# Later bank sums and rests, residual rows over two passes, and a dt chain in steps, in a Trainium2 decoder layer

## The chip, the cores and the metric

The kernel runs on one core of one Trainium2 chip. The metric is the device time of one launch in microseconds, the median of the runs. Before the change it is 1476.61 us (three runs, 1475.93 to 1481.21).

## The reference, cut to what matters

One layer for 1024 tokens of width 1024, all in float32. `h = layer_norm(x)`; one wide projection `h @ w_in` gives the pieces that feed two mixers side by side:

```python
y_a = (silu(z_a) * b_gate * conv3(c_gate * u)) @ w_a_out
xbc = silu(conv4(xbc) + bias);  dt = softplus(dt_raw + dt_bias)
y_s = ssd_chunked(xs, dt, -exp(a_log), bs, cs) + d_skip * xs     # state-space scan, chunks of 128
y_s = gated_group_rmsnorm(y_s, z_s, norm_s_g) @ w_s_out          # four groups of channels
mixed = sigmoid(g_a) * y_a + sigmoid(g_s) * y_s
out = layer_norm(2**0.25 * h + mixed @ w_o) * ln_g + ln_b
```

## The kernel before, in words

Each float32 product is made of three matmuls: an operand is split into a rounded part ("hi") and a rest ("lo"), and hi*hi, hi*lo and lo*hi add up in a PSUM bank (L786 to L788, L922 to L924). ScalarE writes the hi part of a weight block (`prep_hi`, L276), VectorE its lo part by a subtraction (`prep_lo`, through the helper `sub_split`, L106).

The work is one hand-written list of **items**, each one block product on TensorE. Items "p" are the input projection: pairs of 128-column blocks, seven products to a pair. The first three pairs are interleaved and make up the early part; from item 21 (`START`) on, pairs follow one another, and the steps of the scan are placed between them. Items "a" (16) multiply by `w_a`. Items "s" multiply by `w_s`: four groups g of eight products j, written (g, j) below, 24 matmuls of 128x512 each. For every j the four groups add up in the SBUF tile `acc[j]`. After the list comes the output projection with `w_o` (`project`), whose left operands `M[j, half]` are made from `acc[j]` in group 3; what follows the list is not pinned, and the compiler's scheduler may place it among the last items.

For each item n the main loop issues, in this order: the load of the raw weights of item n+5 on SP's queue (`fetch`, L225); hi of item n+3 and lo of item n+2; the product; what stands in `sums[n]`; what stands in `later[n]`. From `START` on `pin` fixes each engine's order to this order of writing. So an instruction that waits holds back all that is written behind it on its engine, and a DMA that waits for its buffer holds back the rest of its queue. There are three lo buffers and eight raw buffers.

What the change touches:

- `item_s` (L850) makes the product (g, j) in two banks of a ring of eight and then empties them: in group 1 by an addition into `acc` (L874), in group 2 by that addition, a product with the tile `sg` (L876) and the addition of `yg` (L877), for each half; in group 3 by L880 and L881, after which ScalarE and VectorE write M (L883, L106). This emptying is called E(g, j) below.
- `load_gy` (L814) loads `sg` and `yg` of product j+1 in product j of group 2; `prep_y` (L770, L772) loads the tiles `rb` and `gt` of a later left operand. These are 512 KB each, and all take buffers of one pool, tag "O", which has four; a load waits on SP's queue until one comes free.
- `prep_y` puts its work two items later: VectorE scales `gt` (L775), ScalarE writes the two hi halves (L764), VectorE the two rests (L106, in `halves`).
- `residual(s)` makes one of eight row blocks of `2**0.25 * h` again: SP loads `x` (L838); one item later ScalarE normalises it (L844), GpSimd multiplies and adds (L845, L846) and stores the row to DRAM through its own queue (L847). Two buffers take turns. Row j is made in product (1, j).
- `item_a` multiplies its two banks with `sga` (L804) and stores the tile one item later.
- `dt_values` makes softplus, the sums over each chunk (L482 to L488 on TensorE) and their exponentials. It is issued whole at item 19, in the early part.

Of the kernel before, what the change touches and what calls it, by code (L numbers as in the profile page):

```python
# [21 lines left out]
AF = mybir.ActivationFunctionType  # L22
ALU = mybir.AluOpType
# [5 lines left out]
KT = D // P  # L29
HALF = 512  # L30
# [15 lines left out]
def trunk_kernel(ctx: ExitStack, tc: tile.TileContext, x, w_in, w_dt, w_a, w_s, w_o, par, con,  # L46
# [58 lines left out]
    def sub_split(lo, full, hi, eng):  # L105
        return eng.tensor_tensor(lo, full, hi.bitcast(F32), ALU.subtract)  # L106
# [46 lines left out]
    def bank(tag, name):  # L153
        return pa.tile([P, HALF], F32, tag=tag, name=name, bufs={"U": 2, "yy": 2}.get(tag, 1))
# [15 lines left out]
    def post_unit(name):  # L170
        n_post[0] += 1
        return unit(POST[(n_post[0] - 1) % 28], name)
# [5 lines left out]
    def xp(i):  # L178
        return ("cv", T_X + 2 * i, T_X + 2 * i + 1)

    def zp(i):
        return ("zs", T_ZS + 2 * i, T_ZS + 2 * i + 1)
# [2 lines left out]
    gates = [("ga", T_GA + 2 * i, T_GA + 2 * i + 1) for i in range(4)]  # L185
    gates += [("gs", T_GS + 2 * i, T_GS + 2 * i + 1) for i in range(4)]
    EARLY = 3
    pairs = [zp(0), zp(1), ("cv", T_BM, T_CM), xp(0), gates[0], xp(1)]
    group_at = {0: len(pairs) - 1}
    for g in range(1, G):  # L190
        pairs += [("cv", T_BM + g, T_CM + g), *conv_pairs[2 * g - 2], xp(2 * g), zp(2 * g), *conv_pairs[2 * g - 1],
# [265 lines left out]
        V.tensor_tensor(v, v, trd3[:, :, H:].rearrange("p c h -> p h c"), ALU.add)  # L457
        V.tensor_tensor(v, v, db_t.unsqueeze(2).to_broadcast([P, H, NCH]), ALU.add)

    def dt_values():  # L460
        v, e, s1, s2 = (w4[0][:, i] for i in range(4))

        S.activation(e, v, AF.Abs)
        ex = S.activation(e, e, AF.Exp, bias=0.0, scale=-1.0)
        V.tensor_scalar(s1, e, 2.0, None, ALU.add)
        V.reciprocal(s2, s1)
        V.tensor_tensor(s1, e, s2, ALU.mult)
        V.tensor_tensor(s2, s1, s1, ALU.mult)
        V.tensor_scalar(e, s2, 2.0 / 17.0, 2.0 / 15.0, ALU.mult, ALU.add)
        for d in (13, 11, 9, 7, 5, 3, 1):  # L470
            V.tensor_tensor(e, e, s2, ALU.mult)
            V.tensor_scalar(e, e, 2.0 / d, None, ALU.add)
        V.tensor_tensor(e, e, s1, ALU.mult)
        V.tensor_scalar(v, v, 0.0, None, ALU.max)
        V.tensor_tensor(dt_t, v, e, ALU.add)

        with tc.issue_after(ex.ins):
            S.activation(al_t, al_t, AF.Exp)
        V.scalar_tensor_tensor(s1, dt_t, -1.0, al_t.unsqueeze(2).to_broadcast([P, H, NCH]), ALU.mult, ALU.mult)
        s1f = s1.rearrange("p h c -> p (h c)")  # L480
        pc1 = bank("tr", "pc1")
        PE.matmul(pc1[:, 0:256], lhsT=upper, rhs=s1f, start=True, stop=True)  # L482
        PE.matmul(pc1[:, 256:512], lhsT=slow, rhs=s1f, start=True, stop=True)
        cumf = cum_t.rearrange("p h c -> p (h c)")
        V.tensor_copy(cumf, pc1[:, 0:256])
        S.activation(dte_t.rearrange("p h c -> p (h c)"), pc1[:, 256:512], AF.Exp)
        pc2 = bank("st", "pc2")
        PE.matmul(pc2[:, 0:256], lhsT=ones, rhs=s1f, start=True, stop=True)  # L488
        S.activation(cdec_t.rearrange("p h c -> p (h c)"), pc2[:, 0:256], AF.Exp)
        for i in range(2):  # L490
            PE.transpose(pc2[:, 256 + i * P:256 + (i + 1) * P], cumf[:, i * P:(i + 1) * P], ident)
        ce = cv("ceT")
        cT, eT = (ce[:, i * 256:(i + 1) * 256].rearrange("p (i l) -> p i l", i=2) for i in range(2))
        V.tensor_copy(cT.rearrange("p i l -> p (i l)"), pc2[:, 256:512])
        S.activation(eT.rearrange("p i l -> p (i l)"), pc2[:, 256:512], AF.Exp)
        for i in range(2):
            rows = slice(i * 16, (i + 1) * 16)
            SP.dma_start(cum_d[rows, :].rearrange("h (c l) -> (h c) l", c=NCH), cT[:, i, :])
            SP.dma_start(ecum_d[rows, :].rearrange("h (c l) -> (h c) l", c=NCH), eT[:, i, :])

    kept, taken = {}, set()
# [252 lines left out]

    ya_raw, Y, acc, sga, M, WO = {}, {}, {}, {}, {}, {}

    def halves(s, k, src):

        for hf_i in range(2):
            u = Y[s, k, hf_i] = post_unit(f"{s}_{k}{hf_i}")
            part = src[:, hf_i * HALF:(hf_i + 1) * HALF]
            S.activation(u[:, 0, :], part, AF.Copy)  # L764
            sub_split(u[:, 1, :], part, u[:, 0, :], V)

    def prep_y(g, k):

        rb = otile(f"rb{g}_{k}")
        SP.dma_start(rb, rst_d[g].squeeze(0).partition_broadcast(P))  # L770
        y = otile(f"gt{4 * g + k}")
        SP.dma_start(y, gat_d[g][:, k, :])  # L772

        def work():
            V.scalar_tensor_tensor(y, y, pc(C_NG + 4 * g + k), rb, ALU.mult, ALU.mult)  # L775
            halves(f"y{g}", k, y)
        later.setdefault(now[0] + (2 if items[now[0]][0] == "s" else 1), []).append(work)

    n_bank = [0]
# [11 lines left out]
    abank = {}  # L791

    def item_a(j, kh, hi, lo):
        if kh == 0:
            sga[j] = otile(f"sga{j}")
            SP.dma_start(sga[j], sga_d[j])
        for hf_i in range(2):
            if kh == 0:
                abank[hf_i] = pbank(f"p_wa{j}_{hf_i}")
            for k in range(4):  # L800
                mm3(abank[hf_i], hi, lo, k, Y["a", 4 * kh + k, hf_i], kh == 0 and k == 0, kh == 1 and k == 3)
        if kh == 1:
            for hf_i in range(2):
                V.tensor_tensor(sga[j][:, hcols[hf_i]], abank[hf_i], sga[j][:, hcols[hf_i]], ALU.mult)  # L804
            later.setdefault(now[0] + 1, []).append(lambda: SP.dma_start(yag_d[j], sga[j]))
        elif 1 <= j < 7:
            prep_y((j - 1) // 4, (j - 1) % 4)

# [41 lines left out]
    def item_s(g, j, hi, lo):  # L850
        if g == 0:
            acc[j] = xtile(j, f"acc{j}") if j < 7 else cv("acc7")
        ps = [pbank(f"p_ws{g}_{j}_{i}") for i in range(2)]
        for hf_i in range(2):
            for k in range(4):
                mm3(ps[hf_i], hi, lo, k, Y[f"y{g}", k, hf_i], k == 0, k == 3)
        if g < 3 and j in (1, 3, 5, 7)[:4 if g < 2 else 2]:
            y_next = 4 * g + 6 + j // 2
            prep_y(y_next // 4, y_next % 4)
        if g == 1:  # L860
            residual(j)
        if g == 1 and j == KT - 1:
            load_gy(0)
        if g == 2 and j < KT - 1:
            load_gy(j + 1)
        if g == 2 and j == KT - 1 or g == 3 and j < KT - 1:
            load_gy((j + 1) % KT, ("sg",))
        for hf_i in range(2):
            sl = hcols[hf_i]
            part = acc[j][:, sl]  # L870
            if g == 0:
                S.activation(part, ps[hf_i], AF.Copy)
            elif g < 3:
                V.tensor_tensor(part, ps[hf_i], part, ALU.add)  # L874
                if g == 2:
                    V.tensor_tensor(part, part, gy["sg", j][:, sl], ALU.mult)  # L876
                    V.tensor_tensor(part, part, gy["yg", j][:, sl], ALU.add)  # L877
            else:
                sg = gy["sg", j][:, sl]
                V.tensor_tensor(sg, ps[hf_i], sg, ALU.mult)  # L880
                V.tensor_tensor(part, part, sg, ALU.add)  # L881
                u = M[j, hf_i] = post_unit(f"m{j}_{hf_i}")
                S.activation(u[:, 0, :], part, AF.Copy)  # L883
                sub_split(u[:, 1, :], part, u[:, 0, :], V)
        if g == 3:
            if j < 4:
                split_wo(j, 0, unit(POST[8 + j], f"wo{j}_0"))
            if 1 <= j < 5:
                split_wo(3 + j, 0, xtile(j - 1, f"wo{3 + j}_0", F32R, (P, 2, HALF)))
            if j == 5:  # L890
                for n, i, src in (("lg", 4, ln_g), ("lb", 5, ln_b)):
                    norm_t[n] = xtile(i, n)
                    SP.dma_start(norm_t[n], src.partition_broadcast(P))
# [73 lines left out]
    for n, it in enumerate(items):  # L967
        if it[0] == "p" and it[2] == 1:
            first_of[n] = it[1]
    START = 7 * EARLY  # L970
    for n, (kind, i, j) in enumerate(items):
        now[0] = n
        for k in range(n, n + LF + 1):
# [15 lines left out]
        if kind == "p":  # L989
            item_p(i, j, hi, lo)  # L990
            if n == 2 * EARLY - 1:
                dt_project(0)
                second_half()
            if n == 3 * EARLY - 1:
                quarter_sums()
            if n == 4 * EARLY + 1:
                dt_project(1)
                dt_turn()
            if n == START - 2:
                dt_values()  # L1000
            if n == START - 1:
                est.release()
                sd["p"] = tc.alloc_tile_pool(name="S", bufs=1, reuse_waits="tile")
        elif kind == "a":
            item_a(i, j, hi, lo)
        else:
            item_s(i, j, hi, lo)
        for f in sums.pop(n, ()):
            f()
        for f in later.pop(n, ()):  # L1010
# [138 lines left out]
```

## Time and profile before

| | before |
|---|---|
| median of three runs | 1476.61 us |
| the profiled execution's own time | 1475.75 us |
| its span, first to last instruction | 1473.9 us |
| mean granted TensorE clock | 0.983 |
| busy TensorE / VectorE / ScalarE / GpSimd | 95 / 69 / 49 / 33 % |

The profiled execution is 0.86 us below the median, and 1.85 us of its time lie outside the span. Times inside it count from the first instruction. PE is TensorE, PEld its weight loads, DVE VectorE, ACT ScalarE, POOL GpSimd, SPq the DMA issues of SP's queue. A group of instructions is named by its line, engine and tiles (output, then inputs); "x2" is two instructions in one line of the view. A bracket in the timeline says how long the engine stood idle before, and what ended that.

### The profile page before, as it was taken

What the parts mean: (1) busy time and instruction counts of PE and PEld (TensorE: products, weight loads), DVE (VectorE), ACT (ScalarE), POOL (GpSimd) and SP (SyncE); (2) the same over time, 40 slices, a digit from 0 to 9 for tenths busy, and PEclk for the clock granted to TensorE, in tenths of its full rate; (3) what the DMA queues carried; (4) which work ended last, traced back from release to release, by engine and by line L of the source; (5) the groups of instructions that cost most, each with busy time, mean ns of one, the idle gap of its engine ahead of it and who ended that gap; (6) DMA issues with size and microseconds to landing.
All of it is one profiled execution on the core that took longest, in us unless ns stands there. A gap on an engine that the chain in (4) does not pass through costs nothing.

```text
span 1473.9 us, 18618 instructions
## 1 busy us (share of the span) xinstructions
PE 1399.5 (95%) x6522; PEld 1104.6 (75%) x6522; DVE 1017.1 (69%) x1495; ACT 717.2 (49%) x1244; POOL 481.9 (33%) x374
## 2 busy tenths in 40 slices
PE   6999999999999999999999999999799998679997
PEld 4677878787777877778787777877588886457886
DVE  7977578877788787697877586675534347668843
ACT  3665466555665645665555665555521332102411
POOL 4012334534334453244444254343000007400054
PEclk9999999999999999999999999999999999889999
DMA  6022255463444545454654535454557445557431
GB/s 228 16 93 100 105 143 134 135 167 112 146 122 141 167 121 133 137 147 122 176 126 143 150 106 166 132 144 146 204 186 242 166 164 198 209 186 243 164 114 57
DMA packets 171901, 217.02 MB, mean 147 GB/s; under 512 B 11520, under 2 KB 116896, under 8 KB 171808
## 3 DMA queue, kind: packets, MB, share of 16 engines
q1 hardware_dynamic: 162128, 181.80, 42.2%
q10 hardware_dynamic: 8272, 29.81, 5.2%
q0 software_dynamic: 1408, 4.23, 0.8%
q8 instruction: 51, 0.84, 0.2%
q14 instruction: 42, 0.34, 0.1%
HBM read 160.97 MB, written 54.82 MB: 146 GB/s over the span
## 4 chain that ended last, share of the span: by engine, by line
PE 79%; DVE 9%; DMA 5%; ACT 2%; POOL 2%; issue 2%; ACTq 0%; POOLq 0%; SPq 0%; DVEq 0%
PE p L922 10%; PE p L924 10%; PE p L923 10%; PE pU L924 8%; PE pU L922 8%; PE pU L923 8%; PE ya L653 2%; PE p_wa L788 2%; PE p_wa L787 2%; PE p_wa L786 2%; PE p_wo L1043 2%; PE p_wo L1045 2%; PE p_wo L1044 2%; PE st L658 2%; PE yb L648 2%
## 5 line engine op out<-in xcount | busy, mean ns | idle before, releaser
L106 DVE TENSOR_TENSOR wlop<-raw_a,whip 128x512 fp32r<-128x512 f32 x210 | 180.7, 861 | 181.2 <-ACT whip L276 67.5
L276 ACT ACTIVATE whip<-raw_a 128x512 fp32r<-128x512 f32 x210 | 127.8, 622 | 43.7 <-issue 10.7
L922 PE MATMUL p<-b,whip 128*128 128x512 f32 x352 | 143.7, 409 | 4.1 <-DVE ob L931 4.1
L922 PE MATMUL pU<-t,whip 128*128 128x512 f32 x352 | 144.5, 412 | 2.7 <-ACT oa L957 2.7
L922 PE MATMUL p<-t,whip 128*128 128x512 f32 x352 | 141.7, 403 | 1.5 <-DVE oa L931 1.5
L924 PE MATMUL p<-t,wlop 128*128 128x512 f32 x352 | 139.1, 395 | 1.5 <-DVE wlop L106 1.5
L923 PE MATMUL p<-b,whip 128*128 128x512 f32 x352 | 139.8, 397 | 0.1
L924 PE MATMUL pU<-t,wlop 128*128 128x512 f32 x352 | 138.9, 395 | 1.0 <-DVE wlop L106 1.0
L924 PE MATMUL p<-b,wlop 128*128 128x512 f32 x352 | 139.6, 397 | 0.0
L923 PE MATMUL pU<-t,whip 128*128 128x512 f32 x352 | 138.9, 395 | 0.0
L923 PE MATMUL p<-t,whip 128*128 128x512 f32 x352 | 138.9, 394 | 0.0
L788 PE MATMUL p_ws<-y,wlos 128*128 128x512 f32 x256 | 106.6, 417 | 32.6 <-DVE wlos L106 32.5
L638 POOL TENSOR_TENSOR xw<-xd,dte_t 128x256 f32<-128x256 f32 x56 | 46.5, 830 | 257.1 <-DVE xd L624 257.1
L786 PE MATMUL p_ws<-y,whis 128*128 128x512 f32 x256 | 105.0, 410 | 0.0
L787 PE MATMUL p_ws<-y,whis 128*128 128x512 f32 x256 | 104.4, 408 | 0.0
L236 POOL TENSOR_TENSOR s<-raw_a,raw_a 128x512 f32<-128x512 f32 x42 | 69.8, 1662 | 86.4 <-DVE wlop L106 73.7
L250 POOL TENSOR_TENSOR raw_a<-raw_a,s 128x512 f32<-128x512 f32 x42 | 65.9, 1570 | 97.9 <-issue 89.8
L106 DVE TENSOR_TENSOR wlop<-s,whip 128x512 fp32r<-128x512 f32 x84 | 80.2, 966 | 11.8 <-PE p L924 8.7
L922 PEld LDWEIGHTS p<-b,whip 128*128 128x128 f32 x352 | 66.7, 190 | 27.1 <-issue 8.6
L788 PEld LDWEIGHTS p_ws<-y,wlos 128*128 128x128 f32 x256 | 50.6, 198 | 48.6 <-DVE wlos L106 36.6
L604 ACT ACTIVATE em<-em,cum_t 128x128 f32<-128x128 f32 x256 | 81.3, 390 | 7.0 <-ACT ob L548 4.1
L922 PEld LDWEIGHTS pU<-t,whip 128*128 128x128 f32 x352 | 66.0, 187 | 19.9 <-ACT oa L957 4.0
(224 smaller groups left out, 3321.2 us busy)
## 6 DMA issues: line engine op xcount, KB each, us to landing
raw_a<-in_w_in_dram SPq DMA_DIRECT2D x168, 256.0 KB
em<-cum_d SPq DMA_DIRECT2D x64, 256.0 KB
xg_d<-cv ACTq DMA_DIRECT2D x16, 512.0 KB
xT<-xg_d SPq DMA_DIRECT2D x32, 256.0 KB
z<-zs_d SPq DMA_DIRECT2D x32, 256.0 KB
gat_d<-y SPq DMA_DIRECT2D x32, 256.0 KB
rb<-rst_d SPq DMA_DIRECT2D x16, 512.0 KB
gt<-gat_d SPq DMA_DIRECT2D x16, 512.0 KB
```

Source lines behind the costliest of these rows:

```text
L106: return eng.tensor_tensor(lo, full, hi.bitcast(F32), ALU.subtract)
L236: Gp.tensor_tensor(s1, r["a21"], r["a22"], ALU.add)
L250: Gp.tensor_tensor(a12, a12, s1s[p]["s2"], ALU.subtract)
L276: S.activation(flat(hi), src, AF.Copy)
L604: S.activation(em[:, h, :], em[:, h, :], AF.Relu, bias=cum_t[:, 8 * g + 4 * i + h, c:c + 1], scale=-1.0)
L638: Gp.tensor_tensor(xw, XD[n, i], dte_t[:, hs, c].unsqueeze(2).to_broadcast([P, HG, HD]), ALU.mult)
L786: PE.matmul(ps, lhsT=hi[:, k, :], rhs=u[:, 0, :], start=start, stop=False)
L787: PE.matmul(ps, lhsT=hi[:, k, :], rhs=u[:, 1, :], start=False, stop=False)
L788: PE.matmul(ps, lhsT=lo[:, k, :], rhs=u[:, 0, :], start=False, stop=stop)
L922: PE.matmul(ps, lhsT=hi[:, k, :], rhs=u[:, 0, :], start=first, stop=False, skip_group_check=True)
L923: PE.matmul(ps, lhsT=hi[:, k, :], rhs=u[:, 1, :], start=False, stop=False, skip_group_check=True)
L924: PE.matmul(ps, lhsT=lo[:, k, :], rhs=u[:, 0, :], start=False, stop=(k == 3), skip_group_check=True)
```

## The change

The third of the first six pairs becomes a pair of gates and the B/C pair takes the next place. `dt_values` becomes a generator with steps, one per item from item 21 on. `halves` can issue its two rests one item later, and `prep_y` asks for that. The product with `sga` in `item_a` and the emptying in `item_s` move into `sums` of the next item, except for the last product, (3, 7), which is still emptied in its own; the store of `sga` moves one item on as well. `residual` is called in every other product of groups 1 and 2 in place of every product of group 1.

```diff
@@ -185 +185 @@
-    pairs = [zp(0), zp(1), ("cv", T_BM, T_CM), xp(0), gates[0], xp(1)]
+    pairs = [zp(0), zp(1), gates[0], ("cv", T_BM, T_CM), xp(0), xp(1)]
@@ -460 +460 @@
-    def dt_values():
+    def dt_steps():
         v, e, s1, s2 = (w4[0][:, i] for i in range(4))
...
         S.activation(e, v, AF.Abs)
-        ex = S.activation(e, e, AF.Exp, bias=0.0, scale=-1.0)
+        S.activation(e, e, AF.Exp, bias=0.0, scale=-1.0)
+        S.activation(al_t, al_t, AF.Exp)
+        yield
...
+        yield
-        for d in (13, 11, 9, 7, 5, 3, 1):
+        for i, d in enumerate((13, 11, 9, 7, 5, 3, 1)):
             V.tensor_tensor(e, e, s2, ALU.mult)
             V.tensor_scalar(e, e, 2.0 / d, None, ALU.add)
+            if i % 2:
+                yield
...
+        yield
+        yield
-        pc1 = bank("tr", "pc1")
+        pc1, pc2 = bank("tr", "pc1"), bank("st", "pc2")
...
+        yield
...
@@ -759 +765 @@
-    def halves(s, k, src):
+    def halves(s, k, src, rest_later=False):
+        parts = [src[:, hf_i * HALF:(hf_i + 1) * HALF] for hf_i in range(2)]
+        us = [post_unit(f"{s}_{k}{hf_i}") for hf_i in range(2)]
         for hf_i in range(2):
...
+            Y[s, k, hf_i] = us[hf_i]
+            S.activation(us[hf_i][:, 0, :], parts[hf_i], AF.Copy)
+        def rests():
+            for u, part in zip(us, parts):
+                sub_split(u[:, 1, :], part, u[:, 0, :], V)
+        if rest_later:
+            later.setdefault(now[0] + 1, []).append(rests)
+        else:
+            rests()
...
-            halves(f"y{g}", k, y)
+            halves(f"y{g}", k, y, True)
@@ -800 +814 @@
         if kh == 1:
-            for hf_i in range(2):
-                V.tensor_tensor(sga[j][:, hcols[hf_i]], abank[hf_i], sga[j][:, hcols[hf_i]], ALU.mult)
-            later.setdefault(now[0] + 1, []).append(lambda: SP.dma_start(yag_d[j], sga[j]))
+            banks = dict(abank)
+            def gate():
+                for hf_i in range(2):
+                    V.tensor_tensor(sga[j][:, hcols[hf_i]], banks[hf_i], sga[j][:, hcols[hf_i]], ALU.mult)
+            sums.setdefault(now[0] + 1, []).append(gate)
+            later.setdefault(now[0] + 2, []).append(lambda: SP.dma_start(yag_d[j], sga[j]))
@@ -857 +875 @@
-        if g == 1:
-            residual(j)
+        if g in (1, 2) and j % 2 == 0:
+            residual(4 * (g - 1) + j // 2)
...
-        for hf_i in range(2):
-            sl = hcols[hf_i]
-            part = acc[j][:, sl]
+        def evac():
+            for hf_i in range(2):
+                sl = hcols[hf_i]
+                part = acc[j][:, sl]
...
+        if g == 3 and j == KT - 1:
+            evac()
+        else:
+            sums.setdefault(now[0] + 1, []).append(evac)
@@ -996 +1020 @@
-            if n == START - 2:
-                dt_values()
...
+        if n == START - 1:
+            dt_work = dt_steps()
+        if n >= START and dt_work is not None and n != first_cv:
+            if next(dt_work, "done") == "done":
+                dt_work = None
         for f in sums.pop(n, ()):
             f()
```

## Rows read from the trace of the kernel before

**Rows 1.** The page: busy time, share of the span and instructions of TensorE and VectorE.
```profile
PE 1399.5 (95%) x6522; PEld 1104.6 (75%) x6522; DVE 1017.1 (69%) x1495; ACT 717.2 (49%) x1244; POOL 481.9 (33%) x374
```

**Rows 2.** Whom TensorE waited for, whole run: total us, times, longest us.
```profile
PE p_ws L788 <- DVE wlos L106: 32.5, 8, 10.9
...
PE pc L482 <- DVE w L479: 2.8, 1, 2.8
```

**Rows 3.** Busy time by stretch, items "s" alone: us, busy by engine, clock, DMA.
```profile
1153.46:1243.06 89.60, 89.60 (x384) 72.19 (x384) 8.06 (x12) 9.57 (x16) 1.00 0.51 174
1243.06:1379.17 136.11, 101.81 (x385) 78.52 (x383) 21.69 (x32) 0.00 (x0) 0.87 0.61 210
```

**Rows 4.** Whom SP's queue waited for, 1190 to 1350 us.
```profile
SPq L838 <- DMA res_d<-rs: 56.4, 6, 21.9
```

**Rows 5.** Timeline of SP's queue: start, us, line, transfer.
```profile
1202.01 0.43 SPq L225 DMA_DIRECT2D raw_s<-in_w_s_dram  x1
1224.36 0.33 SPq L838 DMA_DIRECT2D rs<-in_x_dram  x1
...
1266.49 1.02 SPq L814 DMA_DIRECT2D sg<-sgs_d  x1
```

**Rows 6.** Timeline of VectorE in group 2.
```profile
1274.04 1.47 DVE L876 TENSOR_TENSOR acc<-acc,sg 128x512 f32<-128x512 f32 x1 [9.31 <-DMA sg<-sgs_d]
...
1280.23 0.68 DVE L106 TENSOR_TENSOR wlos<-raw_s,whis 128x512 fp32r<-128x512 f32 x1
...
1295.82 0.69 DVE L877 TENSOR_TENSOR acc<-acc,yg 128x512 f32<-128x512 f32 x1 [1.08 <-DMA yg<-yag_d]
...
1298.48 0.69 DVE L106 TENSOR_TENSOR wlos<-raw_s,whis 128x512 fp32r<-128x512 f32 x1
```

**Rows 7.** The chain that ended last: start, us waited for the landing, transfer.
```profile
1266.49 7.46 DMA sg<-sgs_d
...
1290.90 4.83 DMA yg<-yag_d
...
1298.59 5.51 DMA yg<-yag_d
```

**Rows 8.** Timeline of GpSimd and VectorE where residual rows are made.
```profile
1254.56 2.91 POOL L845 TENSOR_TENSOR rs<-rs,ag 128x1024 f32<-128x1024 f32 x1 [1.40 <-ACT rs L844]
1255.91 4.91 DVE L106 TENSOR_TENSOR y<-gt,y 128x512 fp32r<-128x512 f32 x2 [0.70 <-ACT y L764]
1257.55 2.73 POOL L846 TENSOR_TENSOR rs<-rs,ab 128x1024 f32<-128x1024 f32 x1
...
1263.65 2.74 POOL L846 TENSOR_TENSOR rs<-rs,ab 128x1024 f32<-128x1024 f32 x1
1264.06 0.68 DVE L874 TENSOR_TENSOR acc<-p_ws,acc 128x512 f32<-128x512 f32 x1
```

**Rows 9.** Groups of GpSimd, 1030 to 1380 us: count, busy us, mean ns, idle before.
```profile
L846 POOL TENSOR_TENSOR rs<-rs,ab 128x1024 f32<-128x1024 f32 x8 | 22.3, 2784 | 0.6
L845 POOL TENSOR_TENSOR rs<-rs,ag 128x1024 f32<-128x1024 f32 x8 | 19.6, 2450 | 185.1 <-ACT rs L844 185.1
```

**Rows 10.** Timeline: the steps between an emptied bank and a residual row.
```profile
1242.86 1.24 ACT L844 ACTIVATE rs<-rs,nb_t,rs_t 128x1024 f32<-128x1024 f32 x1 [0.32 <-DMA rs<-in_x_dram]
...
1287.60 1.28 DVE L775 SCALAR_TENSOR_TENSOR gt<-gt,par_t,rb 128x1024 f32<-128x1024 f32 x1
...
1288.91 1.15 ACT L764 ACTIVATE y<-gt 128x512 fp32r<-128x512 f32 x2 [15.85 <-DVE gt L775]
```

**Rows 11.** Timeline of VectorE: the lo parts of (3, 3) and (3, 7).
```profile
1344.64 0.68 DVE L106 TENSOR_TENSOR wlos<-raw_s,whis 128x512 fp32r<-128x512 f32 x1
...
1373.02 0.69 DVE L106 TENSOR_TENSOR wlos<-raw_s,whis 128x512 fp32r<-128x512 f32 x1
```

**Rows 12.** Busy time by stretch, VectorE alone, around the dt chain.
```profile
93.00:112.20 19.20, 17.35 (x33) 1.00 0.25 97
```

**Rows 13.** Busy time by stretch, all engines (TensorE, loads, VectorE, ScalarE, GpSimd), group 2.
```profile
1257.00:1304.00 47.00, 31.80 (x120) 24.22 (x120) 27.43 (x29) 5.71 (x8) 15.11 (x9) 0.85 0.61 216
```

More of the change, by code (lines that the diff above doesn't have):

```diff
@@ L458, in dt_turn @@
         V.tensor_tensor(v, v, db_t.unsqueeze(2).to_broadcast([P, H, NCH]), ALU.add)
-    def dt_values():
+    def dt_steps():
         v, e, s1, s2 = (w4[0][:, i] for i in range(4))
+        s1f = s1.rearrange("p h c -> p (h c)")
+        cumf = cum_t.rearrange("p h c -> p (h c)")
         S.activation(e, v, AF.Abs)
-        ex = S.activation(e, e, AF.Exp, bias=0.0, scale=-1.0)
+        S.activation(e, e, AF.Exp, bias=0.0, scale=-1.0)
+        S.activation(al_t, al_t, AF.Exp)
+        yield
         V.tensor_scalar(s1, e, 2.0, None, ALU.add)
@@ L475, in dt_values @@
         V.tensor_tensor(dt_t, v, e, ALU.add)
-        with tc.issue_after(ex.ins):
-            S.activation(al_t, al_t, AF.Exp)
         V.scalar_tensor_tensor(s1, dt_t, -1.0, al_t.unsqueeze(2).to_broadcast([P, H, NCH]), ALU.mult, ALU.mult)
-        s1f = s1.rearrange("p h c -> p (h c)")
-        pc1 = bank("tr", "pc1")
+        yield
+        yield
+        pc1, pc2 = bank("tr", "pc1"), bank("st", "pc2")
         PE.matmul(pc1[:, 0:256], lhsT=upper, rhs=s1f, start=True, stop=True)
         PE.matmul(pc1[:, 256:512], lhsT=slow, rhs=s1f, start=True, stop=True)
-        cumf = cum_t.rearrange("p h c -> p (h c)")
+        PE.matmul(pc2[:, 0:256], lhsT=ones, rhs=s1f, start=True, stop=True)
         V.tensor_copy(cumf, pc1[:, 0:256])
         S.activation(dte_t.rearrange("p h c -> p (h c)"), pc1[:, 256:512], AF.Exp)
-        pc2 = bank("st", "pc2")
-        PE.matmul(pc2[:, 0:256], lhsT=ones, rhs=s1f, start=True, stop=True)
         S.activation(cdec_t.rearrange("p h c -> p (h c)"), pc2[:, 0:256], AF.Exp)
+        yield
         for i in range(2):
@@ L495, in dt_values @@
         S.activation(eT.rearrange("p i l -> p (i l)"), pc2[:, 256:512], AF.Exp)
+        yield
         for i in range(2):
@@ L499, in dt_values @@
             SP.dma_start(ecum_d[rows, :].rearrange("h (c l) -> (h c) l", c=NCH), eT[:, i, :])
+        yield
     kept, taken = {}, set()
@@ L757, in trunk_kernel @@
     ya_raw, Y, acc, sga, M, WO = {}, {}, {}, {}, {}, {}
-    def halves(s, k, src):
+    def halves(s, k, src, rest_later=False):
+        parts = [src[:, hf_i * HALF:(hf_i + 1) * HALF] for hf_i in range(2)]
+        us = [post_unit(f"{s}_{k}{hf_i}") for hf_i in range(2)]
         for hf_i in range(2):
[L762 to L765, printed above, removed]
+            Y[s, k, hf_i] = us[hf_i]
[7 more added lines that the diff above has]
+            rests()
     def prep_y(g, k):
@@ L867, in item_s @@
             load_gy((j + 1) % KT, ("sg",))
-        for hf_i in range(2):
-            sl = hcols[hf_i]
-            part = acc[j][:, sl]
[L871 to L884, printed above, removed]
+        def evac():
+            for hf_i in range(2):
+                sl = hcols[hf_i]
+                part = acc[j][:, sl]
+                if g == 0:
+                    S.activation(part, ps[hf_i], AF.Copy)
+                elif g < 3:
+                    V.tensor_tensor(part, ps[hf_i], part, ALU.add)
+                    if g == 2:
+                        V.tensor_tensor(part, part, gy["sg", j][:, sl], ALU.mult)
+                        V.tensor_tensor(part, part, gy["yg", j][:, sl], ALU.add)
+                else:
+                    sg = gy["sg", j][:, sl]
+                    V.tensor_tensor(sg, ps[hf_i], sg, ALU.mult)
+                    V.tensor_tensor(part, part, sg, ALU.add)
+                    u = M[j, hf_i] = post_unit(f"m{j}_{hf_i}")
+                    S.activation(u[:, 0, :], part, AF.Copy)
+                    sub_split(u[:, 1, :], part, u[:, 0, :], V)
+        if g == 3 and j == KT - 1:
+            evac()
+        else:
+            sums.setdefault(now[0] + 1, []).append(evac)
         if g == 3:
@@ L970, in trunk_kernel @@
     START = 7 * EARLY
+    dt_work, first_cv = None, -1
     for n, (kind, i, j) in enumerate(items):
```

## The prediction

> **What bounds the kernel now.** I read the page first, then TensorE's waits, then the stretch where they lie. TensorE is busy 95% of the span and VectorE 69% [rows 1], so the matmuls are the bound, and a change that adds and removes none can only win back time in which TensorE stands still or is slow. The waits name one place: 32.5 us in 8 waits for the lo part of `w_s` blocks, up to 10.9 us each, and 2.8 us for the dt chain [rows 2]. The stretches price it: the first 16 products of "s" take 89.60 us, 5.60 us each, at clock 1.00; the next take 136.11 us at a mean granted clock of 0.87 for 385 matmuls [rows 3], where 89.6 would do. So up to 46 us lie in groups 2 and 3, more than the 32.5 us of waits, because after a wait part of the matmuls run at 1.2 GHz.
>
> Why is lo late? SP's queue stood 56.4 us behind residual loads that waited for the store of the row two before [rows 4]; between 1202.01 and 1224.36 us, for instance, nothing was issued [rows 5]. Hence `sg` of (2, 0) was asked for at 1266.49 us [rows 5], VectorE stood 9.31 us in E(2, 0), and the lo part behind it came at 1280.23 [rows 6]. From there VectorE lives in a loop: E(2, j) ends and frees the buffers, `sg` and `yg` of j+1 are loaded, E(2, j+1) can run. TensorE's gaps follow the two.
>
> **The change, part by part.**
>
> *Residual rows, groups 1 and 2.* One row costs GpSimd 2.45 + 2.78 = 5.2 us [rows 9], and every other product means 11.2 us between rows, 22.4 us between uses of a buffer. The queue's 56.4 us of waiting goes. Group 2 gets four rows that it did not have; their price is below.
>
> *Emptying one item later.* Both orders wait for the same event. Before, after product n came E(n) and then lo(n+3); now lo(n+3) comes first and E(n) after it. The number of instructions is the same; product m now stands behind E(m-4), through both lo and the ring of eight banks, where it stood behind E(m-3). TensorE gets 5.6 us more of slack, 16.8 in all. Group 1 holds its banks longer and costs nothing, covered by that slack. In "a" `sga` is held one item longer and `gt` too; the four O buffers then let a `gt` load start some 3 us into a product, to be used a product later, and only VectorE waits, which there has two items of lo in hand: 0.
>
> *When E(2, 0) ends.* Product (2, 0) starts at 1243.06 [rows 3] and ends at 1248.7. Its `yg` takes the buffer whose rests are now issued in (2, 0), and row 3's GpSimd work, from about 1243.5 to 1248.7, holds the second of these rests back: VectorE is through at 1250.1, and with 4.83 us for the landing [rows 7] E(2, 0) ends near 1257.6, where it ended at 1280.2 [rows 6].
>
> *One turn of the loop, from E to E.* The landing of `yg` takes 4.83 to 5.51 us [rows 7]; from the wait's end at 1295.82 to the end of E at 1298.48 are 2.66 us [rows 6]: 7.6 us with the queue's step. Where a left operand is made, its rests free the `gt` buffer that the second load needs, two instructions of 0.6 us behind E: 9.3 us, in two turns. The other work (scaling, lo) fits into the landing.
>
> *What a row adds to a turn.* The trace has no row inside this loop, so I bound it. While GpSimd multiplies, VectorE instructions with two SBUF inputs stand: two rests took 4.91 us and got through in and after the gap between GpSimd's two instructions, while an addition from PSUM ran beside GpSimd in 0.68 us [rows 8]. In the new order a row's ScalarE step stands behind the hi halves of an operand: 1.28 + 1.2 + 1.24 us [rows 10] after E, so GpSimd starts 3.9 us after E and is done 9.3 us after it. L877 is ready at 4.9, gets one of its places in the gap, and the last two instructions follow GpSimd: the turn ends at 10.8 us, 3.1 more than without the row. Ends: 0, if GpSimd falls into the landing, and 5.2, if it holds VectorE all through. I take 3.1, which the instructions' places give, in three turns; the fourth row lies in the last turn, which without loads to wait for would take 4.7, and I count 6.5.
>
> Seven turns: 3 x 10.8 + 2 x 9.3 + 7.6 + 6.5 = 65.1 us. E(2, 7) ends at 1257.6 + 65.1 = 1322.7, and lo(3, 3) directly behind it; before, lo(3, 3) came at 1344.64 [rows 11]. That is **22.0 us**. Beside its own 5.60 us a product TensorE is then late by some 18 us, again because of VectorE. In group 3 the VectorE work is the same and is longer than the product: lo(3, 3) to lo(3, 7) took 28.4 us [rows 11] for four products of 5.60. So the 22.0 us reach lo(3, 7).
>
> *The end of group 3.* E(3, 7) is written ahead of E(3, 6), which the change leaves behind product (3, 7). Block 6 of the output projection's left operand comes one emptying later, up to 5.5 us (28.4 / 4, less two or three instructions of 0.6). As the scheduler can do the other blocks first, I charge **2.0**, between 0 and 5.5.
>
> *The dt chain and the first pairs.* VectorE is busy 17.35 of 19.20 us around the chain [rows 12], and TensorE waits 2.85 us at its end. In steps it lies beside products with two items of slack, and the sums come two items after what they read: I gain **2.8**, between -2 (VectorE late at the first normal pairs, which also get the B/C pair) and 2.8. The four DMAs of the sums are issued twenty items before their first use: 0.
>
> Sum: 22.0 - 2.0 + 2.8 = 22.8 us. 1475.75 - 22.8 = 1453.0 for the profiled execution, which stands 0.86 below the median: **1454 us**.
>
> **The rivals.**
>
> *The rows hide (0.22).* GpSimd falls into the landings, 3 x 3.1 less: 1444. For it: a row's 5.2 us is about as long as a landing of 4.83 to 5.51 [rows 7, 9]. Against it: the order above, which lets GpSimd start only as the landing ends. With E(2, 0) on time as well 1437.
>
> *The rows hold VectorE all through (0.15).* 5.2 us in each of four turns: some 8 us more, 1462. For it: 4.91 us for two rests [rows 8]; against it the one instruction that got through in the gap. The Trainium skill, "SBUF — State Buffer", section "Who interferes with whom", says that whichever of the two engines issues first keeps the shared ports for its whole instruction and the other blocks; by that rule alone the price would be this rival's, and the rows above agree but for the gap.
>
> *The queue's wait only moves (0.07).* Group 2 had 12 MB to load (eight times 1.25 for `sg`, `yg` and weights, twice 1 for an operand) and now moves 16 with four rows loaded and stored, while 216 GB/s at a share of 0.61 were moved there [rows 13]. If each of six landings takes 7.46 us, the longest shown [rows 7], 6 x 2.6 = 16 us are lost: 1470. The skill's page "DMA: Bandwidth & Descriptors", section "Latency and other measured facts", gives HBM access as 0.2 us on average and 2 us at high load; by that six landings would lose about 11 us, which no row here shows by itself.
>
> *Slower (0.06).* The same six landings, behind `gt`, `x` and raw loads and across row stores, at 10.5 us: 6 x 5.7 = 34 us, 1487. It decides from 8.6 us a landing, where the gain is gone. Against it: 5.51 us was reached behind `rb` and `gt` [rows 7].
>
> **How the numbers follow.** My forecast has 0.50. Less than 0.5% (7.4 us) is about what a measurement of this kernel can't tell from no change. Forecast, hidden rows and held VectorE are all faster: 0.87; the moved queue is within: 0.07; slower: 0.06. The range runs from the hidden rows with E(2, 0) on time, 1437, to just short of the moved queue, 1468.
>
> **What would show it.** Right: SP's waits for row stores near zero; `sg` of (2, 0) asked for before 1250 us; turns of E(2, j) of 11 and 9 us in alternation; L876 and L877 of 2 to 3 us wherever GpSimd runs; TensorE's waits for lo starting only near (2, 6) and adding up to under 25 us; no wait at L482. Wrong: turns all near 7.6 us, waits of TensorE in group 1, or landings over 7 us. A wait for M at the first matmuls of the output projection would show the order of E(3, 7) and E(3, 6).

## The result and the profile after

The changed kernel took **1456.51 us** (median of 4 runs, 1455.73 to 1457.33), the kernel before beside it 1476.94, which is 20 us less. The ratio on record, worked out over all the runs and not from the two medians, is 0.9856, with a 95% interval of 0.9836 to 0.9877. The profiled execution took 1455.73 us, 20.0 less than that of before and 2.7 more than the 1453.0 that the sum gave for it. In a later set of runs the same kernel stood at 0.9887 (0.9869 to 0.9905), 17 us under the kernel before beside it, so the gain is 17 to 20 us by the medians of the two sets.

The page after, its span and the busy times that answer to [rows 1]:

```profile
span 1454.0 us, 18639 instructions
...
PE 1396.3 (96%) x6522; PEld 1102.6 (76%) x6522; DVE 1022.1 (70%) x1495; ACT 716.0 (49%) x1243; POOL 481.0 (33%) x374
```

The work is the same; what went is time in which TensorE stood or ran slowly. The view of TensorE's waits after, against [rows 2]:

```profile
PE p_ws L802 <- DVE wlos L106: 12.4, 6, 3.6
...
PE p_ws L801 <- DVE y L106: 5.2, 1, 5.2
```

The 32.5 us for lo parts became 12.4, and the 2.85 us for the dt chain are gone. The same stretch as in [rows 12], TensorE, weight loads, VectorE, ScalarE and GpSimd after it:

```profile
93.00:112.20 19.20, 19.20 (x84) 15.48 (x83) 8.17 (x13) 15.71 (x21) 3.56 (x3) 1.00 0.41 163
```

TensorE is busy all through, and VectorE, at 17.35 us before, for 8.17. But there is a wait that before did not have, 5.2 us at product (3, 0) for the rests of the last operand block. By stretch, the first 16 products of "s" and the next 16 (all engines counted), against [rows 3]:

```profile
1151.14:1240.74 89.60, 89.60 (x385) 71.81 (x384) 49.10 (x51) 30.27 (x50) 17.13 (x9) 1.00 0.54 179
1240.74:1356.87 116.13, 98.47 (x386) 76.55 (x385) 88.36 (x115) 30.07 (x49) 28.94 (x15) 0.93 0.64 227
```

The first stretch is the same to the hundredth; the second lost 20.0 us (136.11 to 116.13), its granted clock going from 0.87 to 0.93. "s" itself began 2.3 us earlier, and 2.3 us are given back after it. So the gain lies where the prediction put it.

SP's queue between 1190 and 1350 us, against [rows 4]:

```profile
SPq L832 <- DVE acc L895: 28.4, 6, 6.7
SPq L786 <- DVE y L106: 17.8, 3, 9.6
...
SPq L832 <- DVE y L106: 10.0, 4, 7.8
SPq L856 <- DMA res_d<-rs: 9.7, 2, 5.0
```

The wait for row stores fell from 56.4 to 9.7 us. What the queue waits for now are VectorE's own steps, the emptyings (L895) and the rests (`y`), because these free the buffers that it loads into. The timeline of VectorE, GpSimd and SP shows what became of that (start, us, engine, line, operation; the wait before it in brackets):

```profile
1240.24 0.32 SPq L832 DMA_DIRECT2D sg<-sgs_d  x1
...
1242.62 2.39 POOL L863 TENSOR_TENSOR rs<-rs,ag 128x1024 f32<-128x1024 f32 x1 [5.06 <-ACT rs L862]
...
1242.81 5.56 DVE L106 TENSOR_TENSOR y<-gt,y 128x512 fp32r<-128x512 f32 x2
1245.09 2.73 POOL L864 TENSOR_TENSOR rs<-rs,ab 128x1024 f32<-128x1024 f32 x1
...
1248.39 0.32 SPq L832 DMA_DIRECT2D yg<-yag_d  x1
...
1253.25 0.69 DVE L896 TENSOR_TENSOR acc<-acc,yg 128x512 f32<-128x512 f32 x1 [2.96 <-DMA yg<-yag_d]
...
1259.60 2.38 POOL L863 TENSOR_TENSOR rs<-rs,ag 128x1024 f32<-128x1024 f32 x1 [10.89 <-ACT rs L862]
1261.40 1.15 DVE L896 TENSOR_TENSOR acc<-acc,yg 128x512 f32<-128x512 f32 x1 [2.10 <-DMA yg<-yag_d]
1262.06 2.73 POOL L864 TENSOR_TENSOR rs<-rs,ab 128x1024 f32<-128x1024 f32 x1
1262.46 0.68 DVE L893 TENSOR_TENSOR acc<-p_ws,acc 128x512 f32<-128x512 f32 x1
1263.18 2.17 DVE L895 TENSOR_TENSOR acc<-acc,sg 128x512 f32<-128x512 f32 x1
1265.09 0.60 POOL L865 DMA_DIRECT2D res_d<-rs  x1 [0.30 <-POOL rs L864]
```

`sg` of (2, 0) is asked for at 1240.24 where [rows 5] had 1266.49. Its `yg` has to wait for the two rests of the operand, which GpSimd's row stretches to 5.56 us, so E(2, 0) ends at 1256.0 (predicted: 1257.6). Then the loop runs, landing and emptying in turn, and a row adds to it: a product of two SBUF tiles (L895) takes 2.17 us instead of 0.69 while GpSimd adds, the addition from a bank (L893) still 0.68.

The landings of `yg` that stand in the chain that ended last (start, us waited), against [rows 7]:

```profile
1248.39 4.76 DMA yg<-yag_d
...
1256.02 5.28 DMA yg<-yag_d
...
1267.30 6.56 DMA yg<-yag_d
...
1276.73 4.96 DMA yg<-yag_d
...
1287.98 6.53 DMA yg<-yag_d
...
1308.70 7.81 DMA yg<-yag_d
```

The first is that of E(2, 0); the others belong to the turns to E(2, 1), (2, 2), (2, 3), (2, 4) and (2, 7): the 5 us to turns with a row, the 6.5 us to turns in which an operand block is made, and the 7.81 to the last turn.

### The profile page after: what moved, and what is told of

It is laid out like the page before. It is cut to its first block, busy times and chain, and to the rows that moved or that the text cites. A ratio compares the mean times of both kernels' runs of the same rounds, so it can differ in the third digit from the quotient of the medians.

```text
span 1454.0 us, 18639 instructions
## 1 busy us (share of the span) xinstructions
PE 1396.3 (96%) x6522; PEld 1102.6 (76%) x6522; DVE 1022.1 (70%) x1495; ACT 716.0 (49%) x1243; POOL 481.0 (33%) x374
## 4 chain that ended last, share of the span: by engine, by line
PE 80%; DVE 10%; DMA 5%; ACT 3%; issue 2%; ACTq 0%; SPq 0%; POOL 0%; POOLq 0%; DVEq 0%
PE p L945 10%; PE p L947 10%; PE p L946 10%; PE pU L947 8%; PE pU L945 8%; PE pU L946 8%; DMA yg<-yag_d 3%; PE ya L659 2%; PE p_ws L800 2%; PE p_ws L802 2%; PE p_ws L801 2%; PE p_wa L802 2%; PE p_wa L801 2%; PE p_wa L800 2%; PE st L664 2%
## 5 line engine op out<-in xcount | busy, mean ns | idle before, releaser
L802 PE MATMUL p_ws<-y,wlos 128*128 128x512 f32 x256 | 104.3, 408 | 12.4 <-DVE wlos L106 12.4
L863 POOL TENSOR_TENSOR rs<-rs,ag 128x1024 f32<-128x1024 f32 x8 | 19.5, 2444 | 231.4 <-ACT rs L862 231.4
```

Of the source, the lines that this page charges most:

```text
L802: PE.matmul(ps, lhsT=lo[:, k, :], rhs=u[:, 0, :], start=False, stop=stop)
```

## The experiments

Marks of the profiled executions, in us, used below. "s" starts between 1151 and 1155 us in runs that share everything ahead of it, so the marks count from its first product: when E(2, 0) ended; the seven turns from there to the end of E(2, 7); the start of lo(3, 3) and of lo(3, 7); and the time from lo(3, 7) to the end of the run.

| kernel | E(2, 0) | turns | lo(3, 3) | lo(3, 7) | rest | ratio to before, 95% |
|---|---|---|---|---|---|---|
| before | 126.8 | 58.2 | 191.2 | 219.6 | 102.7 | |
| changed | 104.9 | 66.3 | 171.1 | 199.6 | 105.0 | 0.9856 (0.9836-0.9877) |
| e1 rows alone | 102.0 | 67.2 | 175.2 | 203.6 | 102.7 | 0.9911 (0.9887-0.9935) |
| e2 old rows | 123.1 | 51.2 | 174.2 | 202.7 | 105.4 | 0.9888 (0.9859-0.9916) |
| e3 early alone | 123.5 | 57.4 | 187.0 | 215.4 | 102.7 | 0.9982 (0.9969-0.9995) |
| e4 own tiles | 105.0 | 56.2 | 161.2 | 189.7 | 106.7 | 0.9821 (0.9801-0.9842) |
| e5 no multiply | 105.0 | 54.4 | 159.3 | 187.9 | 104.5 | 0.9796 (0.9779-0.9812) |
| e6 rests at once | 100.2 | 62.2 | 162.4 | 190.9 | 105.1 | 0.9830 (0.9815-0.9844) |
| e7 rows early | 100.2 | 52.7 | 152.9 | 181.3 | 104.8 | 0.9758 (0.9742-0.9773) |
| e8 e7 + own tiles | 100.2 | 40.3 | 140.5 | 168.9 | 109.7 | 0.9702 (0.9687-0.9716) |
| e9 no deferral | 101.9 | 66.3 | 174.3 | 202.7 | 102.7 | 0.9890 (0.9869-0.9911) |
| e10 changed again | 104.9 | 66.5 | 171.3 | 199.8 | 104.8 | 0.9887 (0.9869-0.9905) |
| e11 rests at once again | 100.2 | 63.9 | 164.1 | 192.6 | 104.7 | 0.9823 (0.9803-0.9843) |
| e12 e8 without deferral | 100.1 | 42.6 | 148.6 | 177.0 | 102.7 | 0.9717 (0.9697-0.9737) |

e1 to e4, e5 to e8 and e9 to e12 are three sets, each on one chip beside the kernel before. The changed kernel has two ratios, 0.9856 and 0.9887, which are 4.6 us apart, so a difference of two ratios out of different sets is uncertain by about as much. Its marks in the two sets agree to 0.2 us, those of e6 and e11 to 1.7 us; where the two disagree below, both are given.

**e1: the rows alone**, on the kernel before.

```diff
-        if g == 1:
-            residual(j)
+        if g in (1, 2) and j % 2 == 0:
+            residual(4 * (g - 1) + j // 2)
```

> The kernel before with one part of the change: residual rows in every other product of groups 1 and 2. Theory (the loss was SP's queue standing behind row loads, so that the loop of group 2 began 22 us late; the later emptying and the later rests are not what won the time): the loads of sg and yg for (2, 0) go out before 1250 us, E(2, 7) ends near 1315 us, and most of the gain is there without the other parts: 1452 to 1459 us. Rival (the gain came from the product more of slack that the later emptying gives): under a third of it, 1469 us or more.

12 us of gain, short of the theory and beyond the rival. The queue's wait for row stores fell to 17.8 us and E(2, 0) came 25 us earlier; the rows now inside the loop made its turns 9.0 us longer.

**e2: all but the rows**: the changed kernel with eight rows in group 1 again.

```diff
-        if g in (1, 2) and j % 2 == 0:
-            residual(4 * (g - 1) + j // 2)
+        if g == 1:
+            residual(j)
```

> The changed kernel with one part undone: all eight residual rows in group 1 again. Theory: SP's waits for row stores come back with some 50 us, E(2, 0) ends after 1270 us, and only the dt chain's 2.3 us and a few us of slack are left of the gain: 1466 to 1474 us. Rival (later emptying won the time): at most 1461 us.

The theory that the rows carry the gain fell: 1459.90 us, against 1474.09 for the kernel before beside it, lies where the rival put it. SP's queue stands as before:

```profile
SPq L856 <- DMA res_d<-rs: 53.7, 6, 17.8
```

E(2, 0) is late as ever (123.1), but its turns take only 51.2 us, and the later emptying lets lo(3, 3) follow E(2, 7) directly. Against the changed kernel's 66.3 us it is the rows that are missing from most turns; against the 58.2 us of before, which has them in the same place, it is mostly the deferrals (the early part alone leaves 57.4), and no run says which. So there are two ways to about the same place: asking early and then running a long loop, or asking late and running a short one. The rows' gain (12 us) and that of the rest (14 us) do not add up: together they gave 17 to 20.

**e3: the early part alone**: the dt chain in steps and the other first pairs, put into the kernel before.

```diff
-            if n == START - 2:
-                dt_values()
...
+        if n == START - 1:
+            dt_work = dt_steps()
+        if n >= START and dt_work is not None and n != first_cv:
+            if next(dt_work, "done") == "done":
+                dt_work = None
```

> The kernel before with the dt chain in steps and the other first pairs alone. Theory: TensorE's wait of 2.85 us for the chain's sums goes, nothing else moves: 2.3 us less than before, 1474 to 1475 us. Rival (the B/C pair and the chain make VectorE late at the first normal pairs): no gain, 1477 us or more.

0.9982 (0.9969 to 0.9995): 0.7 to 4.6 us, the theory's size. TensorE has no wait left at the chain. That "s" began 2.3 us earlier in the changed kernel's profile proves little beside it: in e10, the same kernel, it began at 1154.11, later than before.

**e4: the loop's loads in tiles of their own.** From (2, 1) on, `sg` and `yg` of group 2 get tiles in a region that is free by then, so none of these loads waits for E or for rests.

```diff
-        for n in names:
-            gy[n, j] = otile(f"{n}{j}")
+        for i, n in enumerate(names):
+            if len(names) == 2 and j > 0:
+                gy[n, j] = full_unit(POST[(24 + 2 * (j % 4) + i) % 28], f"{n}{j}")
+            else:
+                gy[n, j] = otile(f"{n}{j}")
```

> The changed kernel; sg and yg of products (2, 1) to (2, 7) get eight buffers of their own (operand tiles that are free in group 2) in place of the four shared ones. Theory (group 2 is a loop of landing and emptying, closed by the four buffers): with the loads ahead of their use the landing leaves the loop, VectorE waits for sg and yg under 5 us in all, E(2, 7) ends before 1308 us, and the time falls by 10 to 18 us to 1438 to 1446 us. Rival (the DMA engines are the limit in group 2): landings grow as much as the loads come earlier, 1453 us or more.

The turns fell by 10.1 us, but the rest became 1.7 us longer: 8.2 us by the marks, 5 by the ratios (0.9821 against 0.9856) and 10 against 0.9887, at best the lower end of what was expected. The rival's longer landings did not come: VectorE waits 3.9 us in all for `yg`. With the landings out of the way, the rows come closer together and hold VectorE instead. Its timeline:

```profile
1298.38 6.13 DVE L106 TENSOR_TENSOR y<-gt,y 128x512 fp32r<-128x512 f32 x2
1298.83 2.35 POOL L866 TENSOR_TENSOR rs<-rs,ag 128x1024 f32<-128x1024 f32 x1
1301.26 2.70 POOL L867 TENSOR_TENSOR rs<-rs,ab 128x1024 f32<-128x1024 f32 x1
1301.79 0.79 PE L801 MATMUL p_ws<-y,whis 128*128 128x512 f32 x1 [8.72 <-DVE y L106]
```

The rests of the last operand took 6.13 us beside GpSimd, and TensorE stood 8.72 us for them at (3, 0).

**e5: the loop without GpSimd's arithmetic.** Rows 4 to 7 are loaded, scaled and stored as before; their multiplication and addition are left out.

```diff
-            Gp.tensor_tensor(r, r, norm_t["ag"], ALU.mult)
-            Gp.tensor_tensor(r, r, norm_t["ab"], ALU.add)
+            if s < 4:
+                Gp.tensor_tensor(r, r, norm_t["ag"], ALU.mult)
+                Gp.tensor_tensor(r, r, norm_t["ab"], ALU.add)
```

> The changed kernel; the last four residual rows, those of group 2, are loaded, normalised and stored, but GpSimd's multiplication and addition are left out of them. Theory (GpSimd holds back VectorE's instructions with two SBUF inputs inside the loop): L896 and L895 fall to 0.7 us in every turn, which takes 1.6 to 2.2 us from each of three turns and 3 from the last, so E(2, 7) ends 7 to 9 us earlier and the time is 5 to 9 us below the changed kernel. Rival (the landing sets the turn whatever GpSimd does): 2 us or less.

0.9796 against 0.9856, some 9 us, and 13 against 0.9887; by the marks lo(3, 7) comes 11.7 us earlier. The theory held in kind, and the size is at its upper end or beyond it. The transfers are all still there, so it is the arithmetic that costs. The turn that answers to the one above:

```profile
1262.25 0.69 DVE L897 TENSOR_TENSOR acc<-acc,yg 128x512 f32<-128x512 f32 x1 [1.34 <-DMA yg<-yag_d]
1262.86 0.68 DVE L894 TENSOR_TENSOR acc<-p_ws,acc 128x512 f32<-128x512 f32 x1
1263.58 0.69 DVE L896 TENSOR_TENSOR acc<-acc,sg 128x512 f32<-128x512 f32 x1
```

Both operations on two SBUF tiles are back at 0.69. In the changed kernel's own four rows, one L896 and one L895 each took longer than 0.69 us, by 0.46 + 1.48, then 0.75 + 1.48, 0.17 + 1.43 and 1.51 + 1.48, in all 8.8 us of the 11.9 by which the turns fell. Most of the other 3 us lies in the turns without a row: those of an operand block had `yg` landed after 5.65 and 5.38 us in place of 6.56 and 6.53.

**e6 and e11: the rests at once.** The rests of an operand block are issued right behind its hi halves again; the emptying stays one product later. e11 is the same kernel, beside e10, the changed kernel again.

```diff
-            halves(f"y{g}", k, y, True)
+            halves(f"y{g}", k, y)
```

> The changed kernel with the rests of a left operand issued at once again, the emptying still one product later. Theory (with a row in group 2 the later rests give little, because the buffer that they free is needed only a turn later): the turns behind an operand get 0.5 to 1.5 us shorter, those before it 1 to 2.5 us longer, TensorE's wait of 5 us for the rests of the last operand at (3, 0) goes over into a wait for lo; time within 3 us of the changed kernel. Rival (the later rests are what shortened the loop): 5 us or more slower.

> The changed kernel as it is, beside the runs without one or the other deferral, so that they are compared on one chip: 0.984 to 0.988 of the time before.

> The changed kernel with the rests at once, in more rounds. Theory (the later rests are a loss here: they hold a buffer of the loop for a product longer, and E(2, 0) and the loop of seven turns end 7 us later): 3 to 6 us below the changed kernel in the same job, an interval that leaves zero out. Rival (the difference of before was one between chips): within 2 us.

e6 was 4 us below the changed kernel by the ratios (0.9830 and 0.9856, the intervals overlap). On one chip with more rounds the two intervals are apart: 0.9823 against 0.9887, 9.4 us by the medians (1448.64 and 1458.00), more than the 3 to 6 expected. By the marks from the start of "s" to the end it is 8.6 us for e6 and 7.3 for e11. So one part of the change costs time. VectorE and SP at (2, 0) in e11:

```profile
1241.01 1.29 DVE L106 TENSOR_TENSOR y<-gt,y 128x512 fp32r<-128x512 f32 x2 [0.70 <-ACT y L771]
1242.33 0.32 SPq L832 DMA_DIRECT2D yg<-yag_d  x1
1242.72 2.39 POOL L863 TENSOR_TENSOR rs<-rs,ag 128x1024 f32<-128x1024 f32 x1 [5.09 <-ACT rs L862]
```

The rests are through before GpSimd begins, and `yg` is asked for 89.4 us into "s", where the changed kernel has 97.3 (1248.39). By the table, E(2, 0) ends 4.7 us earlier and the turns take 2.6 us less; the wait at (3, 0) is gone.

**e9: no deferral at all**: the kernel before with the rows of e1 and the early part of e3.

> The kernel before with the rows over two passes and the early part; neither the emptying nor the rests nor the product with sga are moved. From the runs so far (rows alone 0.9911, early part alone 0.9982, changed kernel 0.9856). Theory (the later emptying is worth the product of slack that it gives, some 5.6 us and more): 0.989 of the time before, 4 to 6 us slower than the changed kernel. Rival (the deferrals cost as much as they give once the rows are spread): within 2 us of the changed kernel.

The theory fell: 1458.06 us against 1458.00 for the changed kernel beside it. The table takes it apart. With e9, E(2, 0) is 3.0 us earlier and E(2, 7) 3.2; but in that order E(3, 0) stands between E(2, 7) and lo(3, 3), which comes 6.1 us behind, where in e10 it follows directly; and after lo(3, 7) the order of e9 is 2.1 us shorter. 3.2 - 6.1 + 2.1 = -0.8, no difference that the runs can tell. In the same set e11, which has the later emptying without the later rests, is 9.4 us below e9 (1448.64 and 1458.06) and 9.4 us below e10: what the later emptying gives, the later rests cost. (With the emptying the product with `sga` is moved too; no run separates these two.)

**e7: the rows early.** In the changed kernel the eight rows go to eight slots of groups 0 and 1, and they and the norm's two vectors into tiles that are free then.

```diff
-                t = norm_t[n] = full_unit(POST[20 + i], n)
+                t = norm_t[n] = full_unit(POST[14 + i], n)
...
-        r = full_unit(POST[22 + s % 2], f"rs{s}")
+        r = full_unit(POST[12 + s % 2], f"rs{s}")
...
-        if g in (1, 2) and j % 2 == 0:
-            residual(4 * (g - 1) + j // 2)
+        slots = (0, 2, 4, 5, 7, 9, 10, 12)
+        if 8 * g + j in slots:
+            residual(slots.index(8 * g + j))
```

> The changed kernel with all eight residual rows ahead of group 2: products 0, 2, 4, 5, 7 of group 0 and 1, 2, 4 of group 1, in four operand tiles that are free then. Theory (two costs of the rows, SP's queue ahead of group 2 and GpSimd within it, can both be avoided): E(2, 0) ends near 1253 us, the turns are 7 and 9 us as in the run with old rows, E(2, 7) ends near 1306 us, and the time is 10 to 15 us below the changed kernel, 1440 to 1446 us. Rival (the loop is closed by landings that wait for DMA bandwidth, so less traffic in group 2 is what counts): over 15 us; or the rows only move their cost into groups 0 and 1: under 4 us.

1439.02 us, 0.9758, is 14 us below the changed kernel by 0.9856, 19 by 0.9887 and 18.6 by the marks: more than expected, and "over 15" was the first rival's number. But the marks came as the theory had them, E(2, 0) at 1253.1, turns of 7.5 to 9.4 us but for the last two, E(2, 7) at 1305.9; and that bandwidth was not the limit e8 shows, which drew 246 GB/s in the second half of "s" where e7 drew 221. Ahead of group 2 TensorE does not wait for VectorE, and there the rows cost nothing.

**e8: e7 with the tiles of e4.**

> The run before and own tiles for sg and yg together. Theory: nothing is left in group 2 but VectorE's own work, 45 us for 45 us of TensorE; E(2, 7) ends before 1298 us, TensorE waits for lo under 3 us in group 2, and group 3 is bound by VectorE's 7 us a product: 1432 to 1440 us. Rival (group 3 gives it all back, since VectorE needs 7 us a product there whenever it starts): as the better of the two single edits, 1443 us or more.

**1430.76 us, 0.9702 (0.9687 to 0.9716)**, below the range expected and the fastest kernel here, 45 us under the one before. Its turns take 40.3 us, 5.8 each, and both halves of "s" run at TensorE's pace (the windows begin two matmuls early):

```profile
1151.72:1241.30 89.58, 89.58 (x386) 72.17 (x385) 61.00 (x51) 35.33 (x54) 46.30 (x24) 1.00 0.69 239
1241.30:1331.52 90.22, 90.22 (x388) 72.72 (x387) 77.65 (x118) 26.32 (x46) 0.00 (x0) 1.00 0.68 246
```

GpSimd is at nothing in the second, the granted clock is 1.00, and the loads moved at 246 GB/s beside it: neither the volume nor the landings were a limit once they had room.

**e12: e8 in the order of before**, that is with the early part, the early rows and the tiles of their own, but no deferral.

> The fastest run so far (rows ahead of group 2, own tiles for sg and yg) without any of the three deferrals. Theory (where no landing closes a loop and no row stands in VectorE's way, one product more or less of slack is worth nothing): 1429 to 1433 us, no wait of TensorE for lo over 1 us in groups 2 and 3. Rival (the slack is needed in group 3, where VectorE takes 7 us a product against 5.6): 1436 us or more.

1432.46 us, 0.9717 (0.9697 to 0.9737): the time held; one wait for lo was longer than the 1 us foretold, 1.4 us at (3, 6). Without the loop the deferrals are worth some 2 us by the ratios, which come from two sets and overlap: nothing that these runs can tell from zero.

## Why the prediction was right

*Total.* Predicted were 22.8 us, profiled 20.0: the 22.0 us up to lo(3, 7) became 20.0 (219.6 - 199.6), the 2.0 lost behind it 2.3, the 2.8 of the dt chain 2.3. The terms came out as follows.

*When E(2, 0) ends.* Right, and for the reason given: 104.9 us into "s" against a predicted 104.1 (1257.6 - 1153.46), with 4.76 us for the landing of `yg` against 4.83. The rests held by row 3's GpSimd work show in the 5.56 us above.

*The turns.* 66.3 us against 65.1, out of terms that miss in both directions:

| turn to E(2, j), j | 1 | 2 | 3 | 4 | 5 | 6 | 7 |
|---|---|---|---|---|---|---|---|
| predicted | 10.8 | 9.3 | 10.8 | 9.3 | 10.8 | 7.6 | 6.5 |
| changed | 10.1 | 10.6 | 10.0 | 10.6 | 10.0 | 6.8 | 8.3 |
| e5, no arithmetic | 7.5 | 9.7 | 7.7 | 9.5 | 8.6 | 5.9 | 5.5 |

The plain turn of 7.6 fits the turns of e5 whose row had no arithmetic (7.5, 7.7 and 8.6); the sixth, for which it was put down, took 6.8, as its `yg` was asked for at 1306.63, before E(2, 5) had ended (1307.3). The mechanism of a row was right, GpSimd starting 3.6 us behind E and an instruction of VectorE getting in between its two; but the 3.1 us was too much: the stretched instructions give 1.9, 2.2 and 1.6. In the last turn they give 3.0, and its `yg` took 7.81 us to land; 8.3 came in place of 6.5. **The mis-sized term in the other direction is the turn in which an operand's rests lie**, 9.3: it took 10.6, since `yg`, last in the queue, landed after 6.5 us and not the 4.83 to 5.51 of [rows 7]. In e5 the row's store left 3.7 us before that turn's `sg` (1261.33 and 1265.03), in the changed kernel 1.0 us before it (1265.09 and 1266.10), and VectorE's wait for `sg` went from 3.14 to 4.18 us. That the store slows the loads is what this suggests; no run isolates it. So the sum of the turns is partly luck: single turns were off by up to 1.8 us, and they cancel to 1.2.

*From lo(3, 3) to lo(3, 7).* lo(3, 3) began as E(2, 7) ended (1322.26), as foretold, and lo(3, 7) came 28.5 us after it against 28.4. VectorE's chain sets this pace in every kernel of the table.

*The end of group 3.* 2.3 us against 2.0, but not for the reason given. In seven of the nine kernels with the later emptying the rest after lo(3, 7) is 104.5 to 105.4 us (it is longer in e4 and e8, where VectorE runs further ahead); in the five with the order of before it is 102.7. So the cost belongs to the order. No wait for block 6, which was named for it, showed up. TensorE in before, then in the changed kernel:

```profile
1372.22 0.39 PE L1043 MATMUL p_wo<-wo,m 128*128 128x512 f32 x1
...
1374.04 0.40 PE L788 MATMUL p_ws<-y,wlos 128*128 128x512 f32 x1
```

```profile
1351.47 0.50 PE L802 MATMUL p_ws<-y,wlos 128*128 128x512 f32 x1 [1.38 <-DVE wlos L106]
...
1356.71 0.39 PE L1070 MATMUL p_wo<-wo,m 128*128 128x512 f32 x1
```

In before, eight matmuls of the output projection (`p_wo`, 1.82 us) stand inside product (3, 7), in front of its first matmul with lo; they fill the time in which lo(3, 7) is made. In the changed kernel that time is a wait of 1.38 us, and the eight come after "s". The eight stand inside (3, 7) in all five kernels with the order of before, and in none of the nine with the later emptying. This makes 1.8 of the 2.3 us; why the scheduler places them so was not tried, and that the charge of 2.0 came near is luck.

VectorE and SP show something else behind "s":

```profile
1365.44 0.33 SPq L916 DMA_DIRECT2D lb<-in_ln_b_dram  x1
1365.82 0.42 SPq L832 DMA_DIRECT2D sg<-sgs_d  x1
...
1371.10 0.69 DVE L899 TENSOR_TENSOR sg<-p_ws,sg 128x512 f32<-128x512 f32 x1 [5.69 <-DMA sg<-sgs_d]
```

`lb` waits for a tile that is emptied a product later, and `sg` of (3, 7) is queued behind it, so VectorE stood 5.69 us. TensorE waited 0.25 us for it, as it had other blocks.

*The dt chain.* The 2.85 us of waiting are gone as predicted, and e3 alone measured a gain of 0.7 to 4.6.

*The rivals.* "The rows hide" fell by e5: 9 us is no hiding. "The rows hold VectorE all through" asked for 5.2 us a turn; the rows give 1.6 to 3.0. (Its "some 8 us" come out as 9.7 by its own terms, 3 x 2.1 and 3.4.) The Trainium skill, "SBUF — State Buffer", section "Who interferes with whom", states the lock that the 2.17 us against 0.69 show, and its statement that a VectorE instruction with at most one SBUF input is not held agrees with the 0.68 of the addition from a bank. The timeline shows besides that VectorE gets one instruction in between two of GpSimd: L896 runs from 1261.40 to 1262.55, across the gap at 1262. "The queue's wait only moves" and "slower" asked for landings of 7.46 us each and over 8.6; those of `yg` in the chain are 4.76 to 6.56, but for the last.

*The signs.* `sg` was asked for in time, TensorE's waits for lo started in product (2, 6) and added up to 12.4 us, and no wait at L482 was left. But the turns did not alternate between 11 and 9 us, of the two stretched instructions only L895 took 2 to 3 us in every row, and one landing, the 7.81 us, was longer than the 7 us that stood for "wrong".

*What the prediction did not see* is that the later rests are a loss. It counted their effect on E(2, 0) and on the turns, but as something that the rows bring, not as something that issuing them at once would save. That is why the total could be right while a part of the change works against it: 9.4 us lie in one argument (e11). Nor did it see that there is another way to the same gain: with the rows left where they were, the rest of the change gains 14 us alone (e2).

## What to carry to other kernels

Where two steps feed each other, a load that waits for a buffer and an instruction that frees it, measure the length of one turn and ask of each edit what it does to the turn and to its start; gains computed for edits made alone do not add up. Before a step is put off, look for the load that waits for the buffer it frees: the later rests held back the very next load and lost 9.4 us here, while the later emptying, which frees buffers too, gained as much because lo then goes ahead of it. Work on GpSimd that is not urgent belongs where VectorE has slack, and loads of a loop that is late belong in tiles of their own: with both on top of it the kernel came 45 us below the one before, where the change alone came 17 to 20.

## What had not been expected of the hardware

Eight rows of GpSimd arithmetic cost nothing measurable beside a TensorE-bound stretch (e8: 89.58 us with 46.30 us of GpSimd) and four of them 9 to 13 us beside a VectorE-bound one (e5). The moved volume was no hindrance: e8 drew 246 GB/s at a DMA share of 0.68 with no wait of TensorE, where the kernel before drew 210 at 0.61 [rows 3] and stood. And a short wait costs more than its length: the second stretch shrank by 20.0 us for 14.9 us less of waiting (32.5 to 12.4 + 5.2), as the mean granted clock in it rose from 0.87 to 0.93, and in e8, where nothing waits, it stayed at 1.00.
